# Order of the first loads, the norm's column load, the squares and the warming products at the start of a hybrid decoder block

## The chip, the core and the metric

The kernel runs on one core of a Trainium2 chip. The metric is the device time of one execution in microseconds (us); lower is better. The engines are named as in the profile: PE (TensorE) does the matrix products and PEld its weight loads, DVE (VectorE) and ACT (ScalarE) the elementwise work, POOL (GpSimd) some copies and fills, and SP (SyncE) issues the DMA transfers.

## The reference, cut to what matters

One decoder block over 512 tokens of width 1024, all in float32. Only its beginning is touched by the change:

```
h = rms_norm(x, attn_norm_g)         # x * rsqrt(mean(x*x) + eps) * g
u = h @ w_in
u_sb, u_rw, u_gate = split(u)
q, k, v = heads of u_sb              # 8 heads of 64
o_sb = stick_breaking_attention(q, k, v)
o_rw = rwkv7_time_mix(u_rw, ...)
x = x + (sigmoid gates of u_gate, o_sb @ w_up_sb, o_rw @ w_up_rw) @ w_out
x = x + square(relu(rms_norm(x) @ w_ff1)) @ w_ff2
x = x + sigmoid(rms_norm(x) @ w_ple_gate) * (p @ w_ple_proj)
return rms_norm(x, final_norm_g)
```

## The kernel before, in words

**Products.** Activations lie with the features on the partitions: x is eight tiles of 128 features by 512 tokens, `x_in`. Every float32 operand is cut into two parts, a rounded one (`w_hi`, `h_hi`) and the rest (`w_lo`, `h_lo`). A product over one tile of 128 features is three matmuls, hi by hi (L191), lo by hi (L192) and hi by lo (L193), each 128x128 by 512 columns; `mm3` records them. A unit is 128 output features, so eight tiles and 24 matmuls. ACT makes the hi part of a weight unit (L175, or L221 in `split`), DVE the lo part (L176, or L222).

**The norm.** x is not normalized before the products. `h` is x times the norm's gain (`attn_g`, one of the columns in the small table `cols`), made by ACT (`h_hi`, L348) and DVE (`h_lo`, L349). The factor `rs`, one over the root of the mean square per token, is applied behind the products. For it ACT squares the eight x tiles (L227, L230), DVE adds them up into `ssum` (L232, L234), PE sums over the partitions (L258), ACT does Ln, Exp and Square (L248 to L250), and DVE two more steps (L251, L252). Every `projected` unit (L389, L401, L409) multiplies by `rs`.

**The start.** Warming products on a zeroed tile (L331) keep PE occupied while the first data come. `first_weights(i, part)` loads half a unit of weights and splits it; `first_x(k)` loads one x tile and makes h of it. The first two units, q and k of the first pair of heads, advance together, tile by tile, into two PSUM tiles of the pool `ps_m`. Unit three, v of the first pair, goes into `ps_z`. Units four to six are q, k and v of the second pair. `fetch_to` loads and splits the units that follow; two raw buffers (`w_raw`) and three split ones are in turn, so a load waits until DVE has made the lo part of the unit two before it. Then the transposes of v (L416), the scores (L453 to L455), and for each block of scores the softplus on ACT and DVE: Abs (L458), Exp (L459), Ln (L460), a DVE step (L461), and the split into `sph` and `spl` (L221, L222). Sums over these (L500, L504), an exponential (L505) and the product with v (L492) follow. Projections of later heads are laid between these steps.

**What sets the order.** The program is written in one order, but a scheduler decides the order in which each engine's queue gets its instructions, by their priority and by when its own model has them ready; each engine then works through its queue in that order. `tc.issue_after(x)` puts what its block records behind x on x's engine. All transfers were issued by SP. Eight semaphores are in turn for them, so the ninth waits until the first has landed.

Of the kernel before, what the change touches and what calls it, by code (L numbers as in the profile page):

```python
# [18 lines left out]
P = 128  # L19
T = 512  # L20
D = 1024
KT = D // P
# [63 lines left out]
def tile_block(ctx: ExitStack, tc: tile.TileContext, xT, xt, pT, wts, lora, cols_d, gfin_d, consts_d, out, dbg=None):  # L86
    nc = tc.nc
    act, dve, pool, pe, sync = nc.scalar, nc.vector, nc.gpsimd, nc.tensor, nc.sync
# [3 lines left out]
    def r32(ap):  # L92
        return ap.bitcast(F32)
# [12 lines left out]
    cols = const.tile([P, NCOLS], F32, name="cols")  # L106
# [12 lines left out]
    def col(name, i):  # L119
        return cols[:, COLS[name] + i:COLS[name] + i + 1]  # L120
# [43 lines left out]
    def fetch_to(n, ahead=0):  # L164
        while state["i"] < min(n, len(seq)):
            i = state["i"]
            state["i"] += 1
            load_to(i + 1 + ahead)
            raw = loaded[i] if seq[i][0] != U_FF2 else sources[seq[i]]()
            if seq[i] in homes:  # L170
                hi, lo = homes[seq[i]]()
            else:
                hi = wpool.tile([P, 1024], F32R, name="w_hi")
                lo = wpool.tile([P, 1024], F32R, name="w_lo")
            act.copy(out=hi, in_=raw)  # L175
            dve.tensor_tensor(out=lo, in0=raw, in1=r32(hi), op=ALU.subtract)  # L176
            ready.setdefault(seq[i], []).append((hi, lo))
# [46 lines left out]
    def sum_squares(pool_, src, k, ssum):  # L224

        if k == 0:
            act.activation(out=ssum, in_=src, func=AF.Square)  # L227
            return
        sq = pool_.tile([P, T], F32, name="sq", bufs=2)[:, 0:src.shape[-1]]
        act.activation(out=sq, in_=src, func=AF.Square)  # L230
        if k == 1:
            dve.scalar_tensor_tensor(out=ssum, in0=sq, scalar=NORM_EPS * D / P, in1=ssum, op0=ALU.add, op1=ALU.add)  # L232
        else:
            dve.tensor_tensor(out=ssum, in0=ssum, in1=sq, op=ALU.add)  # L234
# [36 lines left out]
    psm = ctx.enter_context(tc.tile_pool(name="psm", bufs=2, space=PSUM))  # L271
    with ExitStack() as sA:
        h_hi = pa.tile([P, KT, T], F32R, name="h_hi")
        h_lo = pa.tile([P, KT, T], F32R, name="h_lo")
# [41 lines left out]
        with ExitStack() as s1:  # L316
            p1 = s1.enter_context(tc.tile_pool(name="p1", bufs=2))
            ps1 = s1.enter_context(tc.tile_pool(name="ps1", bufs=2, space=PSUM))

            def ps_z():  # L320
                return ps1.tile([P, T], F32, name="ps_z", bufs=5)
# [5 lines left out]
            warm = p1.tile([P, T], BF16, name="warm", tag="sp")  # L327
            pool.memset(warm, 0.0)
            ps = ps_z()
            for _ in range(12):  # L330
                pe.matmul(ps, warm[:, 0:P], warm, start=True, stop=True)  # L331
            sync.dma_start(out=cols, in_=cols_d)
            ssum = p1.tile([P, T], F32, name="ssum", tag="wl")

            raws = [wpool.tile([P, 1024], F32, name="w_raw", bufs=2) for _ in range(2)]
            first_w = [[wpool.tile([P, 1024], F32R, name=n) for n in ("w_hi", "w_lo")] for _ in range(2)]
            xs_in = {}

            def first_weights(i, part):
                cs = slice(part * 512, part * 512 + 512)  # L340
                sync.dma_start(out=raws[i][:, cs], in_=unit(i)[:, cs])
                split(first_w[i][0][:, cs], first_w[i][1][:, cs], raws[i][:, cs])

            def first_x(k):
                x_in = p1.tile([P, 2, T], F32, name="x_in", tag=("sp", "sph", "spl", "wh")[k // 2]) if k % 2 == 0 else xs_in[k - 1][0]
                sync.dma_start(out=x_in[:, k % 2, :], in_=xT[:, k, :])
                xs_in[k] = x_in, x_in[:, k % 2, :]
                act.activation(out=h_hi[:, k, :], in_=xs_in[k][1], func=AF.Copy, scale=col("attn_g", k))  # L348
                dve.scalar_tensor_tensor(out=h_lo[:, k, :], in0=xs_in[k][1], scalar=col("attn_g", k), in1=r32(h_hi[:, k, :]),  # L349
                                         op0=ALU.mult, op1=ALU.subtract)  # L350


            first_weights(0, 0)
            first_x(0)
            first_weights(1, 0)
            for k in range(1, 4):
                first_x(k)
            first_weights(0, 1)
            first_weights(1, 1)
            for k in range(4, KT):  # L360
                first_x(k)
            loaded.extend(raws)
            state["i"] = 2
            for i in range(2):
                ready[seq[i]] = [tuple(first_w[i])]
            fetch_to(3)

            for k in range(KT):
                sum_squares(p1, xs_in[k][1], k, ssum)
            sync.dma_start(out=cst, in_=consts_d[:, 0:NCONST])  # L370
            first = p1.tile([P, 4 * P], F32, name="first", tag="sums", bufs=1)
            sync.dma_start(out=first, in_=consts_d[:, NCONST:NCONST + 4 * P])
# [154 lines left out]
            for _ in islice(v, 1):  # L527
# [6 lines left out]
                              op0=ALU.mult, op1=ALU.add)  # L534
# [24 lines left out]
            parts = {g: {} for g in heads_}  # L559
# [12 lines left out]
        with ExitStack() as s2:  # L572
# [421 lines left out]
            for st in range(HP + 1):  # L994
                parts = [(len(FILL[st]) * KT, filling(FILL[st]))]
# [370 lines left out]
```

## Time and profile before

| | |
|---|---|
| median of 3 runs | 873.17 us (872.13, 873.17, 873.87) |
| the profiled execution's own time | 874.59 us |
| its span, first to last instruction | 872.8 us |
| mean granted TensorE clock | 0.995 of full speed |
| bytes moved by DMA | 95.32 MB, 109 GB/s on average |

The profile is of one execution; its times are microseconds from the first instruction. Its page cuts the span into 40 slices of 21.8 us and gives the busy tenths of each engine in each:

```profile
PE   9999999999999999998999999999999999999995
DVE  7899987896979888666834789858985987697666
ACT  7888887735345253524524465344434533453743
```

The first slices are the part that the change touches: there DVE and ACT are the busiest in the program but for a few slices, while PE is full in nearly all. In a row of the timeline stand the start, the time taken (from the first to the end of the last, where equal rows are merged), engine, line, operation, tiles with the written one first, and in brackets the idle time ahead of it on its engine and what ended it. Matmuls overlap: one of 512 columns shows some 0.39 us but the next starts 0.23 us behind it. In the table by stretches come the stretch, its length, busy time and number of instructions of PE, PEld, DVE, ACT and POOL, the granted clock, the DMA share and GB/s.

### The profile page before, as it was taken

The page shows a single profiled execution, that of the slowest core. Times are in us where ns is not written, and L with a number is a line of the kernel's source. Part 1 is how long each engine was busy: PE and PEld are TensorE (multiplying, and loading weights), DVE is VectorE, ACT ScalarE, POOL GpSimd, SP SyncE. Part 2 cuts the span into 40 slices and gives each one's busy share as a digit, 9 for nine tenths or more (in the row PEclk, how much of TensorE's full clock was granted, in tenths as well). Part 3 has the DMA queues.
Part 4 walks back from the last instruction along what each step waited for, and adds up shares of the span by engine and source line. Part 5 has one row for each costly group of instructions (what it writes and reads, how often), then busy time and mean ns, then how long its engine had stood idle before and what let it go on. Part 6 is the DMA issues. An engine that isn't in the chain of part 4 may idle for free.

```text
span 872.8 us, 13418 instructions
## 1 busy us (share of the span) xinstructions
PE 853.0 (98%) x5182; PEld 687.9 (79%) x5182; DVE 676.7 (78%) x1230; ACT 449.3 (51%) x706; POOL 78.7 (9%) x136
## 2 busy tenths in 40 slices
PE   9999999999999999998999999999999999999995
PEld 6778787877777777776888888888888888888885
DVE  7899987896979888666834789858985987697666
ACT  7888887735345253524524465344434533453743
POOL 1432421003202021010000000000000000000000
PEclk9999999999999999999999999999999999999998
DMA  7212113131221225357735621531252044200422
GB/s 269 97 62 72 62 61 103 54 101 47 73 74 61 86 75 176 102 174 266 272 97 170 240 73 34 186 119 49 87 178 97 25 141 149 97 1 0 171 71 97
DMA packets 32272, 95.32 MB, mean 109 GB/s; under 512 B 3664, under 2 KB 3664, under 8 KB 32208
## 3 DMA queue, kind: packets, MB, share of 16 engines
q1 hardware_dynamic: 32208, 94.46, 32.4%
q8 instruction: 41, 0.67, 0.3%
q14 instruction: 23, 0.19, 0.1%
HBM read 83.96 MB, written 10.49 MB: 108 GB/s over the span
## 4 chain that ended last, share of the span: by engine, by line
PE 74%; DVE 13%; ACT 7%; DMA 3%; issue 2%; SPq 0%; ACTq 0%; DVEq 0%
PE ps_m L191 13%; PE ps_m L193 13%; PE ps_m L192 13%; PE ps_m L208 7%; PE ps_m L206 7%; PE ps_m L207 7%; DVE w_lo L176 2%; DMA w_raw<-in_wts_dram 1%; ACT hx L1039 1%; PE ps_o L492 1%; PE ps_g L898 1%; DVE LX L836 1%; PE ps_z L500 1%; PE ps_s L936 1%; PE ps_c L927 1%
## 5 line engine op out<-in xcount | busy, mean ns | idle before, releaser
L175 ACT CAST w_hi<-w_raw 128x1024 fp32r<-128x1024 f32 x94 | 99.0, 1053 | 175.6 <-PE ps_m L192 114.8
L176 DVE TENSOR_TENSOR w_lo<-w_raw,w_hi 128x1024 fp32r<-128x1024 f32 x94 | 115.2, 1225 | 38.2 <-ACT w_hi L175 37.7
L191 PE MATMUL ps_m<-h_hi,w_hi 128*128 128x512 f32 x320 | 130.7, 410 | 0.0
L192 PE MATMUL ps_m<-h_lo,w_hi 128*128 128x512 f32 x320 | 128.9, 403 | 0.0
L193 PE MATMUL ps_m<-h_hi,w_lo 128*128 128x512 f32 x320 | 127.6, 399 | 0.0
L191 PE MATMUL ps_m<-hx,w_hi 128*128 128x512 f32 x256 | 99.7, 390 | 0.4 <-ACT hx L1039 0.4
L192 PE MATMUL ps_m<-hx,w_hi 128*128 128x512 f32 x256 | 99.6, 390 | 0.0
L193 PE MATMUL ps_m<-hx,w_lo 128*128 128x512 f32 x256 | 99.5, 389 | 0.0
L193 PEld LDWEIGHTS ps_m<-h_hi,w_lo 128*128 128x128 f32 x320 | 60.3, 188 | 11.7
L192 PEld LDWEIGHTS ps_m<-h_lo,w_hi 128*128 128x128 f32 x320 | 60.5, 189 | 11.3 <-DVE h_lo L349 1.1
L191 PEld LDWEIGHTS ps_m<-h_hi,w_hi 128*128 128x128 f32 x320 | 60.7, 190 | 10.5 <-ACT h_hi L348 0.4
L191 PEld LDWEIGHTS ps_m<-hx,w_hi 128*128 128x128 f32 x256 | 48.0, 188 | 10.4 <-ACT hx L1039 0.6
L192 PEld LDWEIGHTS ps_m<-hx,w_hi 128*128 128x128 f32 x256 | 48.1, 188 | 10.2 <-DVE hx L1040 0.2
L193 PEld LDWEIGHTS ps_m<-hx,w_lo 128*128 128x128 f32 x256 | 48.1, 188 | 9.9
L206 PE MATMUL ps_m<-w_hi,fS 128*128 128x512 f32 x128 | 49.8, 389 | 0.0
L207 PE MATMUL ps_m<-w_lo,fS 128*128 128x512 f32 x128 | 49.8, 389 | 0.0
L208 PE MATMUL ps_m<-w_hi,fS 128*128 128x512 f32 x128 | 49.8, 389 | 0.0
L208 PE MATMUL ps_m<-w_hi,fA 128*128 128x512 f32 x96 | 37.3, 389 | 0.0
L206 PE MATMUL ps_m<-w_hi,fA 128*128 128x512 f32 x96 | 37.3, 389 | 0.0
L207 PE MATMUL ps_m<-w_lo,fA 128*128 128x512 f32 x96 | 37.3, 389 | 0.0
L221 ACT CAST fS<-sums 128x256 fp32r<-128x256 f32 (+1 forms) x32 | 19.9, 620 | 33.3 <-DVE sums L1131 33.3
L1204 DVE TENSOR_TENSOR xs<-ps_m,xs 128x512 f32<-128x512 f32 x56 | 35.8, 681 | 0.0
(378 smaller groups left out, 1876.0 us busy)
## 6 DMA issues: line engine op xcount, KB each, us to landing
w_raw<-in_wts_dram SPq DMA_DIRECT2D x98, 512.0 KB, 3.4
gates<-gg SPq DMA_DIRECT2D x16, 256.0 KB, 2.0
x_in<-in_xT_dram SPq DMA_DIRECT2D x8, 256.0 KB, 5.1
tmp<-gates SPq DMA_DIRECT2D x8, 256.0 KB, 4.2
upsb<-tmp SPq DMA_DIRECT2D x8, 256.0 KB, 2.8
ga<-upsb SPq DMA_DIRECT2D x8, 256.0 KB, 6.3
gb<-gates SPq DMA_DIRECT2D x8, 256.0 KB, 5.8
xs<-in_xt_dram SPq DMA_DIRECT2D x4, 512.0 KB, 7.8
```

Source lines behind the costliest of these rows:

```text
L175: act.copy(out=hi, in_=raw)
L176: dve.tensor_tensor(out=lo, in0=raw, in1=r32(hi), op=ALU.subtract)
L191: pe.matmul(ps, wh, xh[:, k, t], start=first, stop=False)
L192: pe.matmul(ps, wh, xl[:, k, t], start=False, stop=False)
L193: pe.matmul(ps, wl, xh[:, k, t], start=False, stop=last)
L206: pe.matmul(ps, xh[:, k + j], wh, start=first and j == 0, stop=False, skip_group_check=True)
L207: pe.matmul(ps, xh[:, k + j], wl, start=False, stop=False, skip_group_check=True)
L208: pe.matmul(ps, xl[:, k + j], wh, start=False, stop=last and j == 1, skip_group_check=True)
L221: act.copy(out=hi, in_=src)
L492: pe.matmul(ps_o[:, j * P:T], vv[:, j, hh, :, :].rearrange("p a d -> p (a d)"), part[:, ZB[j]:ZB[j] + ZN[j]], start=j == 2 and part is wh, ...
L500: pe.matmul(zt[b][:, :n], tri, part[:, s:s + n], start=False, stop=False, skip_group_check=True)
L1204: dve.tensor_tensor(out=xb, in0=pss[t2], in1=xb, op=ALU.add)
```

## The change

Six edits, all in the stage that starts the program:

- eight warming products instead of twelve;
- the table of columns is issued by ACT's queue instead of SP's;
- x tile 0 is asked for ahead of the weights; the first two units of weights come as pieces of 2, 2 and 4 tiles (128, 128 and 256 KB) instead of two halves of 256 KB; x tiles 4 and 5, and 6 and 7, come as one transfer each;
- the third unit's load and split (`fetch_to(3)`) is put behind the last h;
- the squares of tiles 0 to 3 are put behind h of tile 5, those of tiles 4 to 7 behind h of tile 7;
- k of the second pair of heads goes into a `ps_z` tile instead of a `ps_m` one.

```
             ps = ps_z()
-            for _ in range(12):
+            for _ in range(8):
                 pe.matmul(ps, warm[:, 0:P], warm, start=True, stop=True)
-            sync.dma_start(out=cols, in_=cols_d)
+            act.dma_start(out=cols, in_=cols_d)
...
-            def first_weights(i, part):
-                cs = slice(part * 512, part * 512 + 512)
+            def first_weights(i, lo, n):
+                cs = slice(lo * P, (lo + n) * P)
...
-            def first_x(k):
+            def first_x(k, n=1):
...
-                sync.dma_start(out=x_in[:, k % 2, :], in_=xT[:, k, :])
...
+                sync.dma_start(out=x_in[:, k % 2:k % 2 + n, :], in_=xT[:, k:k + n, :])
+                for j in range(k, k + n):
+                    xs_in[j] = x_in, x_in[:, j % 2, :]
+                    parts = (act.activation(out=h_hi[:, j, :], ...),
+                             dve.scalar_tensor_tensor(out=h_lo[:, j, :], ...))
+                return parts
...
-            first_weights(0, 0)
             first_x(0)
-            first_weights(1, 0)
-            for k in range(1, 4):
-                first_x(k)
-            first_weights(0, 1)
-            first_weights(1, 1)
-            for k in range(4, KT):
-                first_x(k)
+            for i in range(2):
+                first_weights(i, 0, 2)
+            first_x(1)
+            first_x(2)
+            for i in range(2):
+                first_weights(i, 2, 2)
+            first_x(3)
+            for i in range(2):
+                first_weights(i, 4, 4)
+            h_some = first_x(4, 2)
+            h_last = first_x(6, 2)
...
-            fetch_to(3)
-
+            with tc.issue_after(h_last[0].ins), tc.issue_after(h_last[1].ins):
+                fetch_to(3)
             for k in range(KT):
-                sum_squares(p1, xs_in[k][1], k, ssum)
+                after = h_some if k < 4 else h_last
+                with tc.issue_after(after[0].ins), tc.issue_after(after[1].ins):
+                    sum_squares(p1, xs_in[k][1], k, ssum)
...
-                    ps = psm.tile([P, T], F32, name="ps_m") if (hp, i) > (1, 0) else ps_z()
+                    ps = psm.tile([P, T], F32, name="ps_m") if (hp, i) > (1, 1) else ps_z()
```

From line 378 on, the changed program's lines are 8 higher than those before (L395 becomes L403, L458 L466, L504 L512).

The scheduler's order at three places. First SP's queue at the program's start, where `w_raw` is a raw weight unit, `x_in` an x tile and `cols` the table of columns; before:

```order
L332 DMA cols<-in_cols_dram 128x74
L341 DMA w_raw<-in_wts_dram 128x512
L346 DMA x_in<-in_xT_dram 128x512
L341 DMA w_raw<-in_wts_dram 128x512
L346 DMA x_in<-in_xT_dram 128x512 x3
L341 DMA w_raw<-in_wts_dram 128x512 x2
L346 DMA x_in<-in_xT_dram 128x512 x4
```

and now:

```order
L341 DMA w_raw<-in_wts_dram 128x256
L346 DMA x_in<-in_xT_dram 128x512
L341 DMA w_raw<-in_wts_dram 128x256
L346 DMA x_in<-in_xT_dram 128x512 x2
L341 DMA w_raw<-in_wts_dram 128x256 x2
L346 DMA x_in<-in_xT_dram 128x512
L341 DMA w_raw<-in_wts_dram 128x512 x2
L346 DMA x_in<-in_xT_dram 128x1024 x2
```

The columns have left SP; a piece of weights, half as large, still stands ahead of x tile 0.

Second, ACT around the norm: squares (`sq`), casts of the units that follow (`w_hi`), and the factor `rs`. Before, from the cast of unit three on:

```order
L175 CAST w_hi<-w_raw 128x1024
L230 ACTIVATE sq<-x_in 128x512 x2
L175 CAST w_hi<-w_raw 128x1024
L248 ACTIVATE rs<-ps_z 128x512
L249 ACTIVATE rs<-rs 128x512
L175 CAST w_hi<-w_raw 128x1024
L250 ACTIVATE nt<-rs 128x512
L175 CAST w_hi<-w_raw 128x1024
```

and now, from the cast of unit four on:

```order
L175 CAST w_hi<-w_raw 128x1024
L230 ACTIVATE sq<-x_in 128x512 x2
L175 CAST w_hi<-w_raw 128x1024
L230 ACTIVATE sq<-x_in 128x512
L175 CAST w_hi<-w_raw 128x1024
L248 ACTIVATE rs<-ps_z 128x512
L249 ACTIVATE rs<-rs 128x512
L250 ACTIVATE nt<-rs 128x512
```

The casts of units five and six now stand ahead of the first step of `rs`; one of them stood between its steps and one behind them. On DVE all seven additions into `ssum` stand behind the last `h_lo`, with the lo parts of units three, four and five among them; three of them stood among the `h_lo` before. On PE, L258 stood behind the seventh product of unit three and stands behind all 24 of it now.

Third, ACT at the first head's scores, in three blocks of 256, 512 and 512 columns (`sp` holds them, `sph` is the hi part). Before:

```order
L458 ACTIVATE sp<-ps_z 128x256
L459 ACTIVATE sp<-sp 128x256
L458 ACTIVATE sp<-ps_z 128x512
L460 ACTIVATE sp<-sp 128x256
L459 ACTIVATE sp<-sp 128x512
L395 CAST qq_407<-qT 64x512
L460 ACTIVATE sp<-sp 128x512
L221 CAST sph<-sp 128x256
L395 CAST qq_408<-qT 64x512
L458 ACTIVATE sp<-ps_z 128x512
L221 CAST sph<-sp 128x512
L221 CAST sums_hi<-sums 128x128
```

and now, behind the three steps of the block of 256 columns:

```order
L466 ACTIVATE sp<-ps_z 128x512
L403 CAST qq_407<-qT 64x512
L221 CAST sph<-sp 128x256
L467 ACTIVATE sp<-sp 128x512
L403 CAST qq_408<-qT 64x512
L468 ACTIVATE sp<-sp 128x512
L466 ACTIVATE sp<-ps_z 128x512
L467 ACTIVATE sp<-sp 128x512
L468 ACTIVATE sp<-sp 128x512
L221 CAST sph<-sp 128x512
L221 CAST sums_hi<-sums 128x128
```

The last block's Exp and Ln now stand ahead of the cast of `sph` of the block before it. On PE, two products of unit six now stand between the transposes of v and the scores, and unit five's 24 products, all but one of which stood behind the scores before, now all stand there.

More of the change, by code (lines that the diff above doesn't have):

```diff
@@ L337, in tile_block @@
             xs_in = {}
-            def first_weights(i, part):
-                cs = slice(part * 512, part * 512 + 512)
+            def first_weights(i, lo, n):
+                cs = slice(lo * P, (lo + n) * P)
                 sync.dma_start(out=raws[i][:, cs], in_=unit(i)[:, cs])
                 split(first_w[i][0][:, cs], first_w[i][1][:, cs], raws[i][:, cs])
-            def first_x(k):
+            def first_x(k, n=1):
                 x_in = p1.tile([P, 2, T], F32, name="x_in", tag=("sp", "sph", "spl", "wh")[k // 2]) if k % 2 == 0 else xs_in[k - 1][0]
[L346 to L350, printed above, removed]
-            first_weights(0, 0)
-            first_x(0)
-            first_weights(1, 0)
-            for k in range(1, 4):
-                first_x(k)
-            first_weights(0, 1)
-            first_weights(1, 1)
-            for k in range(4, KT):
-                first_x(k)
+                sync.dma_start(out=x_in[:, k % 2:k % 2 + n, :], in_=xT[:, k:k + n, :])
+                for j in range(k, k + n):
+                    xs_in[j] = x_in, x_in[:, j % 2, :]
+                    parts = (act.activation(out=h_hi[:, j, :], in_=xs_in[j][1], func=AF.Copy, scale=col("attn_g", j)),
+                             dve.scalar_tensor_tensor(out=h_lo[:, j, :], in0=xs_in[j][1], scalar=col("attn_g", j), in1=r32(h_hi[:, j, :]),
+                                                      op0=ALU.mult, op1=ALU.subtract))
+                return parts
+            first_x(0)
+            for i in range(2):
[9 more added lines that the diff above has]
+            h_last = first_x(6, 2)
             loaded.extend(raws)
```

## The prediction

> **What bounds the kernel now.** I read the page first, for the share of each engine, then the table by stretches, then the timeline of the first 40 us, since the edits end there.
>
> ```profile
> span 872.8 us, 13418 instructions
> PE 853.0 (98%) x5182; PEld 687.9 (79%) x5182; DVE 676.7 (78%) x1230; ACT 449.3 (51%) x706; POOL 78.7 (9%) x136
> ...
> PE 74%; DVE 13%; ACT 7%; DMA 3%; issue 2%; SPq 0%; ACTq 0%; DVEq 0%
> ```
>
> PE (TensorE) is the bound: 98% busy, 74% of the chain that ended last. So a time saved at the start counts if PE runs its products earlier and nothing later makes it wait for the difference.
>
> ```profile
> 50.00:60.00 10.00, 10.00 (x57) 8.42 (x55) 8.93 (x19) 7.52 (x15) 1.72 (x4) 1.00 0.14 54
> ```
>
> From 50 us on PE has no idle time (10.00 of 10.00 us), and behind that point the changed program's order on the engines is the old one. The change is therefore worth what PE gains or loses in the first 50 us. This is what they look like:
>
> ```profile
> 0.73 1.28 ACT L124 ACT_TABLE_LOAD   x1 [0.73 <-PEq L1358]
> 1.18 0.42 SPq L341 DMA_DIRECT2D w_raw<-in_wts_dram  x1
> 1.31 5.30 PE L331 MATMUL ps_z<-warm 128*128 128x512 bf16 x12 [1.31 <-POOL warm L328]
> 1.65 0.42 SPq L346 DMA_DIRECT2D x_in<-in_xT_dram  x1
> 2.14 0.15 PEld L331 LDWEIGHTS <-warm 128*128 128x128 bf16 x1 [0.28 <-issue]
> 2.57 0.15 PEld L331 LDWEIGHTS <-warm 128*128 128x128 bf16 x1 [0.28 <-issue]
> 5.14 0.72 ACT L348 ACTIVATE h_hi<-x_in,cols 128x512 fp32r<-128x512 f32 x1
> 6.05 0.99 PE L191 MATMUL ps_m<-h_hi,w_hi 128*128 128x512 f32 x1
> 7.18 0.40 PE L193 MATMUL ps_m<-h_hi,w_lo 128*128 128x512 f32 x1
> 7.41 0.39 PE L191 MATMUL ps_m<-h_hi,w_hi 128*128 128x512 f32 x1
> 12.96 0.19 PEld L192 LDWEIGHTS ps_m<-h_lo,w_hi 128*128 128x128 f32 x1 [0.43 <-DVE h_lo L349]
> 18.12 0.39 PE L191 MATMUL ps_z<-h_hi,w_hi 128*128 128x512 f32 x1
> ```
>
> The warming products are 0.43 us apart (weight loads at 2.14 and 2.57); from 7.2 us on a product takes 0.23 us from start to start (7.18, 7.41). So TensorE runs at half pace until about 7.0 us. The first real product starts at 6.05, once h_hi of tile 0 is made (5.14 + 0.72 = 5.86); the 48 products of the first two units then run with one notable wait (0.43 us for h_lo at 12.96), and unit three starts at 18.12.
>
> **The change, part by part.** *Start.* On SP a piece of weights still goes ahead of x, against what the change says of itself, but the columns are gone, so x tile 0 is issued one slot (0.47 us: 1.18 to 1.65) earlier, and 128 KB less go before it.
>
> ```profile
> 9.00:10.00 1.00, 1.00 (x6) 0.83 (x5) 1.00 (x3) 1.00 (x3) 0.00 (x0) 1.00 1.04 371
> ...
> cols<-in_cols_dram SPq DMA_DIRECT2D x1, 37.0 KB, 1.9
> x_in<-in_xT_dram SPq DMA_DIRECT2D x8, 256.0 KB, 5.1
> ```
>
> At 371 GB/s these 128 KB are 0.35 us. Tile 0 had landed by 5.14 at the latest, so it lands by 5.14 - 0.47 - 0.35 = 4.3; h_hi takes 0.72, and PE followed it by 0.19 (5.86 to 6.05): first product at 5.25 instead of 6.05. The columns now wait on ACT for the table load (to 2.01) and take 1.9 us: 3.95, in time. Bounds: were they issued during the load, 2.6; were they queued behind the SP transfers like an x tile (5.1), 7.2, and the first product 2 us late. I take 3.95, the row of the same transfer. Eight warming products end at 1.31 + 8 x 0.43 = 4.75 and leave PE idle for 0.5 us; twelve would have held it until 6.4. With the clock released at 7.0 as before, 4 products run at 0.43 until then, and the other 44 take 44 x 0.227 = 10.0: unit three starts near 17.1, which is **1.05 us early** (the wait at 12.96 goes, since no square stands ahead of the last operands on ACT or DVE). Smaller pieces cost a slot each on SP (two more weight pieces), taken back by two x pairs; casts of the same bytes add about 0.1 us each, hidden because PE is behind the operands from tile 1 on. Bounds of this term: 0 (columns or transfers late) to 1.4.
>
> *Norm.* Seven additions into ssum, three of which stood among the operands, now all stand behind the last h_lo on DVE.
>
> ```profile
> 15.41 0.68 DVE L234 TENSOR_TENSOR ssum<-ssum,sq 128x512 f32<-128x512 f32 x1
> 16.02 0.22 DVE L532 CAST ident_b<-cst 128x128 bf16<-128x128 f32 x1
> 16.15 1.21 DVE L176 TENSOR_TENSOR w_lo<-w_raw,w_hi 128x1024 fp32r<-128x1024 f32 x1
> 17.29 0.68 DVE L234 TENSOR_TENSOR ssum<-ssum,sq 128x512 f32<-128x512 f32 x1
> 18.87 0.69 DVE L234 TENSOR_TENSOR ssum<-ssum,sq 128x512 f32<-128x512 f32 x1
> 19.71 1.03 PE L258 MATMUL ps_z<-ssum,cst 128*128 128x512 f32 x2
> 20.78 0.60 ACT L248 ACTIVATE rs<-ps_z 128x512 f32<-128x512 f32 x1 [1.15 <-PE ps_z L258]
> 24.87 0.69 DVE L252 SCALAR_TENSOR_TENSOR rs<-nt,rs 128x512 f32<-128x512 f32 x1
> 25.05 1.05 ACT L175 CAST w_hi<-w_raw 128x1024 fp32r<-128x1024 f32 x1 [1.55 <-DMA w_raw<-in_wts_dram]
> 27.28 0.68 DVE L389 SCALAR_TENSOR_TENSOR qT<-ps_m,rs 128x512 f32<-128x512 f32 x1
> 29.22 0.66 PE L416 MATMUL ps_m<-cst,vT 128*128 128x128 f32 x4 [0.29 <-DVE vT L409]
> ```
>
> An addition advances DVE by 0.61 (15.41 to 16.02), a w_lo by 1.14 (16.15 to 17.29), a small cast by 0.13. h_lo of tile 7 should end at 14.3 (it ended at 15.49). Seven additions, three w_lo and five small casts stand from there to the last addition: 4.3 + 3.4 + 0.7 = 8.4, so ssum is done at 22.8 instead of 19.56. PE gets to L258, now behind all 24 products of unit three, at 17.1 + 24 x 0.227 = 22.5, and starts it at 23.0: a **wait of 0.5 us**, with unit four queued behind it. Then ACT: the cast that waited for its DMA at 25.05 used to stand behind L248 and now stands ahead of it.
>
> ```profile
> 20.99 3.99 DMA w_raw<-in_wts_dram
> ...
> w_raw<-in_wts_dram SPq DMA_DIRECT2D x98, 512.0 KB, 3.4
> ```
>
> Its buffer comes free with the second full w_lo at 19.8 (its DMA was issued at 20.99 before); 3.4 us of transfer and 1.03 of cast bring L248 to 24.2, just behind L258's end at 24.0. From L248's start to rs it was 4.8 us with a cast between; without it, 5 instructions of 0.6 to 0.7 make 3.4: rs at 27.6, 2 us late. But qT had waited until 27.28 behind a w_lo, which now comes earlier: it starts at 27.6 and the transposes of v at 29.7, where PE, with all of unit four done by 29.2, waits 0.5. The same wait is in the row at 29.22 (0.29, counted from the end of the product before; about 0.45 by the pace). This term is **0** (bounds 0 and 1.0, the latter by 3.99 instead of 3.4 and an equal slip of the scores). The third pair's partial sums in ps_z instead of ps_m give PE two products ahead of the scores.
>
> *Scores.* The first head's softplus now runs in another order on ACT.
>
> ```profile
> 31.44 0.36 PE L453 MATMUL ps_z<-qq,kk 128*128 128x256 f32 x1 [0.17 <-DVE kk L405]
> 33.66 0.62 ACT L459 ACTIVATE sp<-sp 128x512 f32<-128x512 f32 x1
> 34.69 0.63 ACT L460 ACTIVATE sp<-sp 128x512 f32<-128x512 f32 x1
> 36.91 0.62 ACT L221 CAST sph<-sp 128x512 fp32r<-128x512 f32 x1
> 37.01 0.47 PE L191 MATMUL ps_m<-h_hi,w_hi 128*128 128x512 f32 x1
> 37.58 0.33 PE L504 MATMUL ps_z<-sph,neg 128*128 128x128 f32 x1
> ```
>
> From the first score to the cast of block 1 it was 5.5 us (31.44 to 36.91). Now Exp and Ln of the last block (0.62 and 0.63, dependent) stand ahead of this cast: some 6.8 us, so 31.7 + 6.8 + 0.6 = 39.1. Ahead of PE's row at L504 (L512 now) stand 20 products and some 4,200 columns of scores and sums, 1.9 us at 0.227 per 512: 31.7 + 4.5 + 1.9 = 38.1. It waits about 1.0 where it waited 0.34 (37.01 to 37.58 for one product); the later blocks slip with it, some 0.3 more. **Loss 1.0** (0.3 to 1.3).
>
> Sum: -1.05 + 0.5 + 0 + 1.0 = +0.45 us. The profiled execution took 874.59 (span 872.8 and 1.8 around it): 875.0. The median of the runs, 873.17, lies 1.4 below this execution, so the same sum gives 873.6.
>
> [...] The rows show half pace until 7.0 us, 5.7 us after the first warming product, and a later return to it:
>
> ```profile
> 403.00:406.40 3.40, 1.31 (x7) 0.88 (x7) 3.16 (x10) 0.64 (x1) 0.00 (x0) 1.00 0.59 217
> 406.40:409.80 3.40, 3.40 (x9) 2.64 (x8) 2.26 (x4) 0.75 (x2) 0.00 (x0) 0.50 0.74 233
> ```
>
> After a stretch with PE busy 1.31 of 3.40 us the granted clock was 0.50 for 3.4 us, then full again. [...]
>
> **Rivals.** (1) *The clock stays at half pace for another 3.4 us*, because the stretch from 3.6 to 7.0 us now has 0.5 us of idle PE in it. Against it: 85% busy; for it: from 0.2 to 3.6 us PE was busy for 67% and the pace stayed low. Eight products instead of 15 run in it, 7 x 0.227 = 1.6 us lost, of which the 0.5 us wait at L258 takes in part: +1.1, 874.7. (2) *Slower: the norm hangs on the weight DMA.* Every us by which the transfer ahead of L248 takes over 3.4 moves rs, qT and the scores, with PE stopped at the transposes. It decides the sign from 4.7 us (0.45 + 1.3 = 1.75); 3.99 was seen, and 6.7 for a transfer of that size queued behind others, but this one is alone in its queue. At 5 us: 875.2. (3) *PE has cover after all*: the scores' new order costs nothing, since more products of units four to six lie between: -1.05 + 0.5 - 0.4 = -0.95, 872.2. (4) *The start isn't gained*: columns or transfers as late as before, PE at unit three at 18.1; L258's wait goes with it: +0.5 on the forecast, 874.1.
>
> **How the numbers follow.** Forecast 873.6 with 0.55 (its own terms give 872.8 to 874.5), rival 1 with 0.12, rival 2 with 0.08, rival 3 with 0.15, rival 4 with 0.10. The three runs before spread over 1.74 us, 0.2%, about what a measurement of this kernel can tell from no change: the bounds are 871.4 and 874.9. Faster: a third of rival 3 and the forecast's edge, 0.07. Slower: rival 2 and a part of 1, 0.13. Same: 0.80. The range, from rival 3 to rival 2, is 872.0 to 875.3.
>
> **What would show it.** In the changed kernel: first L191 at 5.2 (right) or past 6 (rival 4); pace 0.23 from 7.0 or only from 10.4 (rival 1); the first product of unit three at 17.1; a PE wait for DVE ssum at L258 of about 0.5; L248 right behind a cast that waited for its DMA; a PE wait for ACT sph at L512 near 38 to 39. The prediction is wrong if L258 or L512 doesn't wait, or if PE at 50 us stands over 1.5 us away from the old order's place.

## The result, and the profile after

| | before | changed |
|---|---|---|
| median of the runs | 873.28 us | 877.71 us |
| lowest and highest | 872.13, 874.53 | 874.80, 881.72 |
| runs | 15 | 15 |
| the profiled execution | 874.59 us, clock 0.995 | 874.80 us, clock 0.997 |

The changed kernel takes 1.0053 of the time before, 95% interval 1.0043 to 1.0063: 4.4 us slower, outside the predicted range. Its runs spread over 6.9 us, three times as far as those before, and the execution that was profiled is the fastest of them. So the first thing to see is that this profile, taken alone, hides most of the loss. The page of the changed kernel (span, busy times, the queue of instruction fetches, and the chain that ended last):

```profile
span 872.9 us, 13417 instructions
PE 851.9 (98%) x5178; PEld 687.5 (79%) x5178; DVE 678.5 (78%) x1232; ACT 450.6 (52%) x708; POOL 78.7 (9%) x136
...
q8 instruction: 41, 0.67, 0.3%
...
PE 73%; DVE 13%; ACT 7%; DMA 3%; issue 2%; SPq 0%; POOL 0%; ACTq 0%; DVEq 0%
```

Its busy times differ from those before by 0.3% at most. In the stretch from 50 to 60 us PE is busy for 9.56 of 10.00 us, where it was busy all the time before: it waits 0.41 us at 51.35. The stretch, and the timeline of the start, the norm, the first scores and the place near 300 us, with the rows that answer to those in the prediction:

```profile
50.00:60.00 10.00, 9.56 (x49) 7.39 (x50) 9.40 (x18) 7.32 (x14) 3.15 (x5) 1.00 0.17 54
```

```profile
0.73 1.28 ACT L124 ACT_TABLE_LOAD   x1 [0.73 <-PEq L1366]
0.76 0.40 ACTq L332 DMA_DIRECT2D cols<-in_cols_dram  x1
4.25 0.72 ACT L349 ACTIVATE h_hi<-x_in,cols 128x512 fp32r<-128x512 f32 x1 [0.73 <-DMA x_in<-in_xT_dram]
5.02 1.22 PE L191 MATMUL ps_m<-h_hi,w_hi 128*128 128x512 f32 x2
17.67 0.39 PE L191 MATMUL ps_z<-h_hi,w_hi 128*128 128x512 f32 x1
23.59 1.13 PE L258 MATMUL ps_z<-ssum,cst 128*128 128x512 f32 x2 [0.32 <-DVE ssum L234]
23.88 1.05 ACT L175 CAST w_hi<-w_raw 128x1024 fp32r<-128x1024 f32 x1 [2.01 <-DMA w_raw<-in_wts_dram]
24.83 0.59 ACT L248 ACTIVATE rs<-ps_z 128x512 f32<-128x512 f32 x1
39.23 0.60 ACT L221 CAST sph<-sp 128x512 fp32r<-128x512 f32 x1
39.88 0.33 PE L512 MATMUL ps_z<-sph,neg 128*128 128x128 f32 x1 [0.32 <-ACT sph L221]
51.35 0.33 PE L512 MATMUL ps_z<-spl,neg 128*128 128x128 f32 x1 [0.41 <-DVE spl L222]
57.91 0.60 PE L424 MATMUL ps_m<-cst,vT 128*128 128x128 f32 x4
297.34 0.75 PE L820 MATMUL ps_g<-LX,own 32*32 32x32 f32 x64
299.10 0.85 PE L820 MATMUL ps_g<-LX,LB 32*32 32x64 f32 x42
301.56 0.53 PE L820 MATMUL ps_g<-LX,LB 32*32 32x64 f32 x22 [1.60 <-issue]
```

The same late instructions before:

```profile
56.60 0.60 PE L416 MATMUL ps_m<-cst,vT 128*128 128x128 f32 x4
295.97 0.75 PE L812 MATMUL ps_g<-LX,own 32*32 32x32 f32 x64
297.74 1.10 PE L812 MATMUL ps_g<-LX,LB 32*32 32x64 f32 x64
405.09 0.63 PE L979 MATMUL ps_c<-cst,y 128*128 128x128 f32 x4 [2.87 <-DVE y L974]
```

How to read the two together: the lines from 378 on are 8 higher in the changed kernel, so L416 and L424, L812 and L820, L979 and L987 are the same instructions. PE reaches the transposes of the second pair's v at 57.91 instead of 56.60, 1.31 us late, and 64 small products (L820) at 299.10 instead of 297.74, 1.36 us late: nothing is lost or won for 240 us between. They belong to a burst of small products that begins at 297.34, with `own`. Then, inside the group of 64 identical products, PE stands still for 1.60 us, waiting for no other engine ("issue"). Before, the same 64 products ran without a gap. The table of PE's waits in the changed kernel has this stop first:

```profile
PE ps_g L820 <- issue: 1.8, 2, 1.6
...
PE ps_c L987 <- DVE y L982: 1.5, 1, 1.5
...
PE ps_z L512 <- DVE spl L222: 0.4, 1, 0.4
...
PE ps_z L258 <- DVE ssum L234: 0.3, 1, 0.3
PE ps_z L512 <- ACT sph L221: 0.3, 1, 0.3
```

And the second row takes time back: PE waits 1.5 us for y at L987 where it waited 2.87, so that much of its lateness is hidden there.

What stands near 299 us besides is a fetch on the queue `q8 instruction`. The DMA view of the changed kernel for the stretches 293 to 297 and 297 to 301 us (queue, packets, MB, share of 16 engines) has only data in the first and one fetch of 16,384 bytes in the second:

```profile
q1 hardware_dynamic: 250, 0.63, 40.2%
...
q1 hardware_dynamic: 144, 0.52, 41.8%
q8 instruction: 1, 0.02, 1.4%
```

Before, one such fetch stands in the first stretch, at 293.22 us in the trace:

```profile
q1 hardware_dynamic: 188, 0.44, 36.3%
q8 instruction: 1, 0.02, 1.8%
```

Another stands in the second, at 299.00. Over the whole trace of the changed kernel the queue has 41 such fetches (0.67 MB), on average 254 PE instructions apart, with gaps from 117 to 451. That they bring PE's code is inferred from how PE goes on behind them (below). The sixteenth, at 293.22 before, comes at 299.24 in the changed kernel, where PE is 1.36 us late.

### The profile page after: what moved, and what is told of

It is laid out like the page before. It is cut to its first block, busy times and chain, and to the rows that moved or that the text cites. A ratio compares the mean times of both kernels' runs of the same rounds, so it can differ in the third digit from the quotient of the medians.

```text
span 872.9 us, 13417 instructions
## 1 busy us (share of the span) xinstructions
PE 851.9 (98%) x5178; PEld 687.5 (79%) x5178; DVE 678.5 (78%) x1232; ACT 450.6 (52%) x708; POOL 78.7 (9%) x136
## 4 chain that ended last, share of the span: by engine, by line
PE 73%; DVE 13%; ACT 7%; DMA 3%; issue 2%; SPq 0%; POOL 0%; ACTq 0%; DVEq 0%
PE ps_m L191 13%; PE ps_m L193 13%; PE ps_m L192 13%; PE ps_m L208 7%; PE ps_m L206 7%; PE ps_m L207 7%; DVE w_lo L176 2%; DMA w_raw<-in_wts_dram 1%; ACT hx L1047 1%; ACT w_hi L175 1%; PE ps_o L500 1%; PE ps_g L820 1%; PE ps_z L508 1%; PE ps_g L906 1%; DVE LX L844 1%
## 5 line engine op out<-in xcount | busy, mean ns | idle before, releaser
L191 PE MATMUL ps_m<-h_hi,w_hi 128*128 128x512 f32 x312 | 127.7, 411 | 0.3 <-ACT h_hi L349 0.2
L192 PE MATMUL ps_m<-h_lo,w_hi 128*128 128x512 f32 x312 | 125.8, 403 | 0.1
L193 PE MATMUL ps_m<-h_hi,w_lo 128*128 128x512 f32 x312 | 124.7, 400 | 0.0
L192 PEld LDWEIGHTS ps_m<-hx,w_hi 128*128 128x128 f32 x256 | 48.1, 188 | 10.2 <-DVE hx L1048 0.2
```

The costliest lines, as they stand in the source:

```text
L191: pe.matmul(ps, wh, xh[:, k, t], start=first, stop=False)
L192: pe.matmul(ps, wh, xl[:, k, t], start=False, stop=False)
L193: pe.matmul(ps, wl, xh[:, k, t], start=False, stop=last)
```

## The experiments

Three theories stood at the start. **F**: four warming products fewer are eight PE instructions fewer (a weight load and a product each), which shifts where PE's code is fetched against the bursts of small products. **C**: the shorter warming lets the clock be released later or fall back. **S**: the new order around norm and scores costs all of it.

**Warming and number of instructions, crossed.** `a12` is the changed kernel with twelve products:

```
-            for _ in range(8):
+            for _ in range(12):
```

> The changed kernel with twelve warming products instead of eight; nothing else moves on any engine. Measured so far: 877.7 median for the changed kernel, 873.3 for the one before; by their two profiles PE is 1.3 us late from 51 to 298 us, then a further 1.6 us in a burst of small products (L820) where PE waited for nothing but its own instructions. Theory F (instruction fetch: eight PE instructions fewer shift the borders at which PE's code comes in into bursts of small products): the late fetch goes, median 875 +- 0.7. Theory C (clock: with eight products the clock is released a window later in many executions, or half-pace windows come back): that goes, 875 +- 0.7 too, the profile's release near 7.0, and the granted clock of all timed runs 0.995 or more. Theory S (the new order around norm and scores costs it all): 877.5 +- 0.7.

`a8t4` keeps eight and adds four small ones, so that the number of instructions is that of twelve; `b8` and `b8t4` do to the kernel before what the change did to it, without and with the four small ones:

```
             for _ in range(8):
                 pe.matmul(ps, warm[:, 0:P], warm, start=True, stop=True)
+            for _ in range(4):
+                pe.matmul(ps[:, 0:16], warm[:, 0:P], warm[:, 0:16], start=True, stop=True)
```

> The changed kernel with its eight warming products and four more of 16 columns behind them: as many PE instructions as with twelve, but 0.3 us or less of PE's time. Theory F: as with twelve, 875 +- 0.7, and no stop of PE in the burst at L822. Theory C: the clock is as with eight, 877.5 +- 0.7, clocks of the timed runs down to 0.992. Theory S: 877.5 +- 0.7.

> The kernel before with eight warming products instead of twelve; nothing else moves. Theory F: the borders of PE's code shift as in the changed kernel, 1.5 to 3 us more: 875 to 876.3, with a stop of PE inside a burst of small products. Theory C: PE idles from 4.7 to 6.0 us, the clock is released later: 875 to 877, clocks of the timed runs below 0.995 in some. Theory S: 873.3 +- 0.5.

> The kernel before with eight warming products and four of 16 columns behind them: PE's instructions as many as before, the warming as short as in the changed kernel. Theory F: 873.3 +- 0.5. Theory C: 875 to 877, as with eight alone. Theory S: 873.3 +- 0.5.

`a8long` is the cell that was missing: a warming as long as twelve products in as few instructions as eight. A float32 product of 512 columns shows as two records that start 0.44 us apart (L258 before, at 19.71 and 20.15), where the products around it are 0.23 us apart.

```
-            for _ in range(8):
+            warm32 = p1.tile([P, T], F32, name="warm32", tag="sph")
+            pool.memset(warm32, 0.0)
+            for _ in range(4):
                 pe.matmul(ps, warm[:, 0:P], warm, start=True, stop=True)
+            for _ in range(2):
+                pe.matmul(ps, warm32[:, 0:P], warm32, start=True, stop=True)
```

> The changed kernel with a warming as long as twelve products made of fewer instructions: four bf16 products and two f32 ones of 512 columns (which take two passes of twice the length), so that PE is busy to about 6.5 us, but as many PE instructions stand ahead of the first real product as with eight. Theory F (only the place of the code borders counts): as the changed kernel, 877 +- 1, with PE's stop of 1.5 to 2.2 us in the burst at L820 near 299 us. Theory C (the short warming and PE's idle time behind it count): as with twelve, 874 +- 0.6, no stop.

Measured (each ratio to the kernel before on the same chip, whose median lay between 872.2 and 874.2 from one such comparison to the next, so kernels of different rows are compared by ratio; stop: the `issue` wait in the burst near 299 us):

| kernel | instructions ahead | warming | median us | ratio, 95% interval | stop |
|---|---|---|---|---|---|
| changed | 8 fewer | short | 877.71 | 1.0053, 1.0043 to 1.0063 | 1.60 |
| a8t4 | as before | short | 874.30 | 1.0012, 1.0002 to 1.0022 | none |
| a12 | as before | long | 873.87 | 1.0005, 0.9997 to 1.0014 | none |
| a8long | 8 fewer | long | 876.39 | 1.0045, 1.0029 to 1.0060 | 2.0 |
| b8 | 8 fewer | short | 876.95 | 1.0046, 1.0027 to 1.0064 | 1.97 |
| b8t4 | as before | short | 874.47 | 1.0014, 1.0004 to 1.0024 | none |

The time goes with the number of instructions, in both programs, and much less with the warming. By the ratios eight fewer cost 0.41% in the changed program, some 3.6 us, and 0.32%, some 2.8 us, in the one before. Four products' worth of warming costs 0.07% in the first, where the intervals overlap, and 0.14% (1.4 us by the medians) in the second. Theory S falls as the cause of the loss: with twelve products the whole new order is within the measurement of no change. Theory C falls as its main cause, since `a8long` loses about as much with the long warming and `a8t4` little with the short one. F's own numbers were met in `a8t4` and `a8long` and missed elsewhere: `a12` came out 0.4 us under the least that F or C gave, `b8` 0.65 over F's most, within C's range, and `b8t4` 0.7 over F's most. So the warming has a part. In the ten traces with twelve products the clock was released (its first record at full speed) between 5.2 and 7.3 us, in `a8long` at 5.8; with eight it was released at 10.2 and 10.3 us in two of seven (`b8t4` and one execution of the changed kernel), and in `b8` it fell back to half from 8.00 to 11.41 us. In `a12` the burst is one group again, and its fetch is in the first stretch, as before. The timeline of PE and the DMA view from 293 to 297 us of `a12`:

```profile
299.57 1.10 PE L820 MATMUL ps_g<-LX,LB 32*32 32x64 f32 x64
```

```profile
q1 hardware_dynamic: 268, 0.72, 45.5%
q8 instruction: 1, 0.02, 2.0%
```

**Why the changed kernel's other runs are slower still.** Two more executions of it, unchanged:

> The changed kernel itself once more, to see where one of its slower executions loses time against the profiled one (874.8). Theory F: the stop near 299 us comes again and others stand at fetches elsewhere, late ones above all. Theory C: the clock is released near 10 us or falls back to half pace for 3.4 us, 1.4 to 1.7 us each; then the granted clock shows where.

> As the look before it, a third execution: 876 to 880. Theory F: same stop near 299 us. Theory C: a half-pace window in the granted clock that the profiled execution did not have.

They took 877.24 and 877.61 us. Both have the stop, of 2.05 and 1.98 us, and both lose more right behind it. The table by stretches of the second (PE's busy time is the second figure; the clock is the third from the end), with the row in the timeline where PE goes on:

```profile
302.73 0.64 PE L820 MATMUL ps_g<-LX,LB 32*32 32x64 f32 x22 [1.98 <-issue]
```

```profile
299.60:303.02 3.42, 1.44 (x76) 1.21 (x73) 0.93 (x2) 1.16 (x2) 0.00 (x0) 1.00 0.12 46
303.02:306.43 3.41, 3.41 (x74) 2.30 (x66) 1.95 (x4) 1.58 (x2) 0.00 (x0) 0.50 0.08 28
```

the first:

```profile
300.43:303.84 3.41, 1.36 (x72) 1.10 (x66) 0.74 (x2) 1.16 (x2) 0.00 (x0) 1.00 0.09 31
303.84:307.25 3.41, 3.41 (x78) 2.38 (x69) 1.95 (x4) 1.57 (x2) 0.00 (x0) 0.50 0.14 50
```

and the profiled execution from the result, whose clock stayed full:

```profile
296.93:300.35 3.42, 3.02 (x141) 2.40 (x140) 1.58 (x5) 1.12 (x2) 0.00 (x0) 1.00 0.51 158
300.35:303.76 3.41, 2.20 (x71) 1.61 (x72) 2.31 (x5) 1.24 (x3) 0.00 (x0) 1.00 0.02 5
```

The stretches are cut at the release of the clock in each execution (6.06, 10.29 and 6.83 us) and multiples of 3.413 us behind it: a half-clock window was that long before (406.39 to 409.80) and here (303.02 to 306.43, 303.84 to 307.25), and these three began 117, 87 and 86 such lengths behind their releases. Where the stop falls into one window, PE is busy in it for 1.36 or 1.44 us and gets the half clock for the next window, which costs about another 1.1 us of PE's time (the lateness against the kernel before grows from 4.40 to 5.50 us). Where the border of two windows cuts the stop, as in the profiled execution, PE is still busy for 2.20 us of 3.41 in the emptier one, and nothing follows. So in these three executions the half clock came behind the stop, and whether it came went with where the windows lay: by that reading it is a part of the spread from 874.8 to 881.7. The 15 runs go the same way: the seven with a mean clock of 0.996 or 0.997 took 874.80 to 877.71, the seven with 0.992 to 0.994 took 877.72 to 881.72.

**How the fetch comes late.** Two conjectures were set against each other: PE's sequencer reads some instructions ahead and stops at the wait ahead of the burst before it has asked for the code, which is all or nothing (R); or every instruction of shift costs a part (G). `a8t2` is `a8t4` with two small products, `b12t4` the kernel before with four behind its twelve, eight instructions more:

> The changed kernel with two products of 16 columns behind its eight: four PE instructions more than the changed kernel, four fewer than with twelve products. In the kernels that ran well the burst near 297 us began 22 to 28 PE instructions behind the one that PE was starting when the code was fetched near 295 us; with eight fewer it would begin 14 to 17 behind. Theory R (PE's sequencer reads ahead by some 17 to 22 instructions, stops at the burst's wait, and the fetch goes out only when that wait ends): here it is 18 to 21, at the limit; either no stop and 874.3 +- 0.7, or the stop and 877 +- 1, with the fetch at 295 or 299 us to match, and nothing between. Rival G (each instruction fewer costs a part, by contention spread over all fetches): halfway, 875.7 +- 0.4.

> The kernel before with four products of 16 columns behind its twelve: eight PE instructions more, the shift to the other side. Theory R: the fetch near 293 us goes out in the stretch of long products as before, 30 to 36 instructions ahead of the burst; 873.3 +- 0.7, no stop near 297 us. Rival G (any shift from the old alignment costs): 875 to 877.

`a8t2` took 877.93 us, 1.0042 (1.0029 to 1.0055), with the whole stop; `b12t4` 872.28 us, 0.9980 (0.9971 to 0.9990), with none. Of `a8t2`:

```profile
302.26 0.54 PE L822 MATMUL ps_g<-LX,LB 32*32 32x64 f32 x24 [1.61 <-issue]
```

Half the shift costs all of it, and a shift to the other side costs nothing, so G falls. Counted in the traces, the fetch goes out when PE starts the instruction 21 or 23 ahead of the burst's first (L820 with `own`, which waits for DVE and PE) in all twelve traces without a stop, those with eight instructions more among them; in the six with a stop it comes 192 to 276 instructions behind the burst's first, and nothing lies between. In the profiled changed kernel the burst starts at 297.34, a weight transfer of 512 KB runs from 297.55 to 299.65, and the fetch is seen at 299.24. So the fetch is seen either 21 or 23 instructions ahead of the burst or 1.73 to 2.36 us behind its first product, with the burst already running, as R has it; where the border of the code lies no trace shows.

Two more things in the six fit that PE stands still for this code: it goes on 2.3 to 2.4 us behind the start of the fetch in each, and 4,245 PE instructions stand ahead of the place where it stopped (4,247 in `b8`), in `a8t2` too, whose burst begins four instructions later. One number of R was missed: it had the fetch of `b12t4` 30 to 36 instructions ahead of the burst, and it came 21 ahead, as without the eight more. So eight instructions more did not move its place against the burst. In the twelve it stands 0.93 to 1.20 us behind PE's small product at L927 (by the lines of the kernel before), which also waits for a semaphore and is 34 instructions ahead of the burst; in the six it stands 1.73 to 2.36 us behind the burst's own first product. That speaks for R's account, in which the end of a wait lets the fetch go, in both cases; the reading ahead itself is not shown. How much of the delay is the transfer's no run tells, since none moved it. The stop of 1.6 to 2.1 us stands beside the 1.10 us that all 64 products take without it.

**What of the order costs, and what hides it.** Two parts of the change undone in `a12`: `a12sq` records the squares as before, `a12ps` has k of the second pair in `ps_m` again.

```
-                after = h_some if k < 4 else h_last
-                with tc.issue_after(after[0].ins), tc.issue_after(after[1].ins):
-                    sum_squares(p1, xs_in[k][1], k, ssum)
+                sum_squares(p1, xs_in[k][1], k, ssum)
```

```
-                    ps = psm.tile([P, T], F32, name="ps_m") if (hp, i) > (1, 1) else ps_z()
+                    ps = psm.tile([P, T], F32, name="ps_m") if (hp, i) > (1, 0) else ps_z()
```

> The changed kernel with twelve warming products and the squares recorded as before (not put behind h): shows in the trace how much of the 1.9 us by which PE is late from 55 us on is theirs. If the squares' place is the cause, PE stands within 0.5 us of the kernel before at 60 us; if it is the two PSUM tiles or the fetch, it stays at 1.5 to 2.

> The changed kernel with twelve warming products and k of the second pair back in a ps_m tile: the other part. If the PSUM tile is the cause, PE is within 0.5 us of the kernel before at 60 us; if the squares' place is, it stays at 1.5 to 2 us.

One execution each took 872.79 and 875.78 us. Their starts differ (unit three at 19.10 and 18.73; the three of the changed kernel differ by 1.3 us there), so PE's way from unit three to the transposes of the second pair's v is compared. Before it is 18.12 to 56.60 (38.48 us), in the changed kernel 17.67 to 57.91 (40.24), in `a12` 18.32 to 58.52 (40.20), in `a12sq` 19.10 to 57.41 (38.31) and in `a12ps` 18.73 to 59.88 (41.15). So the order costs 1.7 to 1.8 us there, and without the squares' place nothing is left of it. Other traces bear that out: the two further programs with the squares as before (`a12sqy`, `a12sqyt`, below) have 38.31 and 38.16, the five others with the order of before 37.87 to 38.82, the other two executions of the changed kernel 40.27 and 40.81. The 0.9 us by which `a12ps` is longer don't show that the PSUM tile helps: `a8long`, which has the tile, took 41.49, and 1.4 us of `a12ps` are a wait for `ssum` at L258.

These 1.8 us do not reach the end in `a12` (1.0005). The wait for y at L979 was meant to show why: ACT's copies of y stand there behind sigmoids that wait for their DMAs (in the kernel before ACT is idle for 4.32 us ahead of L662 at 388.38). `by` (from the kernel before) and `a12y` (from `a12`) put the copies ahead:

```
-                    act.copy(out=y[HALVES[odd]], in_=psy[odd]...)
+                    copy = act.copy(out=y[HALVES[odd]], in_=psy[odd]...)
+                if hp == HP - 1:
+                    state["norm"] = copy
```

> The kernel before, with ACT's copies of the last y (L958) put ahead of the two sigmoids of tmp (L662) and the one of gb (L1075), which wait there for their DMAs; PE's order is untouched. In the kernel before, PE stands still for 2.9 us at L979 for y. Theory H (what is lost before 400 us is hidden by this wait, since y hangs on these DMAs and not on PE): the copy goes early, the wait shrinks by 2 us or more, 870.5 to 871.8 against 873.2. Rival N (y hangs on PE's own chain, the wait stays): 873.2 +- 0.5.

> The changed kernel with twelve warming products and the same move of y's copies. With twelve products PE was 1.9 us late from 55 to 298 us and yet the time came out 0.8 above the kernel before or less. Theory H: with the wait for y gone the 1.9 us count: 1.5 to 2.2 us above the kernel before with the same move. Rival N: as far apart as without the move, 0.4 to 0.8.

`by` took 872.68 us, 0.9991 (0.9981 to 1.0001), `a12y` 874.12 us, 1.0006 (0.9994 to 1.0017). In `by` the wait has shrunk by 2.5 us, as H said:

```profile
404.41 0.63 PE L981 MATMUL ps_c<-cst,y 128*128 128x128 f32 x4 [0.38 <-DVE y L976]
```

0.38 us of it are left. The gain of 0.7 us is half of the least that H forecast, and its interval reaches no change; the two kernels now stand 1.4 us apart where `a12` and the kernel before stood 0.8: in the direction of H, below its 1.5, and within the intervals of either. That the wait hides lateness is shown by the traces alone (2.87 us before, 1.46 in the changed kernel, 0.73 in `a12`); that it hides all of the 1.8 us is not settled.

**A version that beats both.** `a12sqy` joins `a12sq` and the moved copies. `byt` and `a12sqyt` are `by` and `a12sqy` with four small products more.

> A version meant to beat both: the changed kernel with twelve products, the squares as before, and the last y's copies put ahead of the sigmoids on ACT. The look at the kernel with the squares alone gave 872.8, with PE 0.8 us late at 55 us after a late start. Without a stop and with the wait for y shortened: 872.0 to 872.8, 0.7 to 1.3 under the kernel before. If the wait for y only moves on, 872.8 to 873.3.

> The kernel before with both moves that helped it: four products of 16 columns behind the twelve (0.998 of the kernel before by itself) and the last y's copies ahead of the sigmoids (0.999). If the two add up: 0.9965 to 0.9975. If one covers the other (with the code fetch on time PE is back at the wait for y): 0.998.

> The best version so far (the changed kernel with twelve products, the squares as before, the last y's copies moved: 0.9979 of the kernel before) with the same four small products behind the twelve. If the shift helps here as it did the kernel before: 0.9965 to 0.9975. If its gain there was the wait for y, which is gone here already: 0.998.

`a12sqy` took 872.34 us, 0.9979 (0.9969 to 0.9988), `byt` 872.14 us, 0.9987 (0.9975 to 0.9999), `a12sqyt` 871.39 us, 0.9978 (0.9968 to 0.9988). The gains don't add up: what `b12t4` won alone (0.9980) is not won again on top of the moved copies, and neither `byt` nor `a12sqyt` came to the 0.9965 to 0.9975 that a sum would have given. The best are 0.2% under the kernel before: the changed kernel with its first loads and PSUM tile, but twelve warming products, the squares where they were, and y's copies moved.

## Why the prediction was wrong

Forecast 873.6, range 872.0 to 875.3; measured 877.71.

- **The step that failed**: "behind that point the changed program's order on the engines is the old one. The change is therefore worth what PE gains or loses in the first 50 us." The order is the old one, but not the place of the program in PE's stream of code: with eight instructions fewer in the first microseconds a fetch 300 us later stood in a burst (299.24) and no longer in a stretch of 0.23 us products (293.22 before). The prediction counted four warming products as 1.7 us of PE's time and never as instructions. It failed a second way too, with the other sign: at L987 the wait for y hides lateness of the first 400 us (1.46 us are left of 2.87), so a term of the first 50 us is not worth its size at the end.
- **Start, -1.05**: -0.45 in the profiled execution (17.67 against 18.12), +0.88 and -0.21 in the other two. The first product came at 5.02, even before the forecast 5.2, but 0.3 us of the lead was lost among the first products, which ran at half pace (0.43 us from 6.04 to 6.47, 0.23 from 7.11 on), one of them after a wait of 0.2 us for `h_lo`, and more at the x pairs near 12 us. The columns didn't wait for ACT's table load (0.73 to 2.01): ACT's queue issued them at 0.76, as the bound that was put aside had it. They took 2.5 us, not 1.9, and landed at about 3.3, with no effect, since x tile 0 landed last (`h_hi` waited for it until 4.25). Two casts of 256 columns took 0.80 us on ACT (0.41 and 0.39) where one of 512 took 0.62.
- **Clock** (rival 1, 0.12): released at 6.83 in the profiled execution, but at 10.29 in one of the other two, with unit three 1.3 us later. There the idle time was longer than the 0.5 us that the prediction had: PE was busy for 2.47 of 3.42 us in the window that ended 3.41 us ahead of the release. That idle time in such a window holds the clock back was the author's conjecture; no run shows it alone. The late release itself came in a part of the executions and has a part in the spread; what the medians showed of the warming is 0.4 us in this program (`a12` against `a8t4`), within the noise.
- **Norm, 0.5**: the wait at L258 is 0.32 and L248 stands right behind the cast that waited for its DMA, at 24.83 (forecast 24.2). Right in the profiled execution; in the other two the wait was 0.4 and 0.9. The 14.3 us at which the last `h_lo` should end was given without its working; it ended at 14.92.
- **Scores, +1.0**: `sph` of the second block ended the wait at 39.88, but for 0.32 us. PE's ten products more ahead of it (2.27 us at 0.227) account for nearly all of 39.88 against 37.58. The longest wait came one block later, at 51.35 for `spl` (0.41), where the prediction had 0.3 for all later blocks. Idle time of PE between unit three and the transposes at 57.91 grew only by 0.53 us (1.36 for 0.83); the rest of the 1.76 is products that start further apart, whose cause was not followed. So the size came out, the place and the mechanism only in part.
- **Sum at 50 us, +0.45**: +1.31 at 57.91, below the 1.5 that was named as the point of failure; the other two executions stand at +2.7 and +2.1, above it. 0.60 of the difference is the start (-0.45 for -1.05), the rest the norm and the scores (1.76 for 1.5).
- **From there to 877.7**: the execution of 877.61 was 2.2 us late ahead of the burst; the stop added 2.2 and the half clock 1.1 (5.5 us in all); the shorter wait for y, 1.69 instead of 2.87, took back 1.2. That leaves 4.3 us at L987, near the 4.4 between the medians. Behind it the profiled execution before loses another 1.6 us in a half-clock window at 406 us (in the prediction's rows), which the changed kernel's three traces don't have. That the median run before is without this window is likely, as it is 1.3 us faster than the profiled one, but no trace shows it.
- **The chances**: "slower by over 0.2%" had 0.13, by a mechanism (the weight DMA) that did not occur: the transfer ahead of L248 took 3.37 us (forecast 3.4).

## What to carry to other kernels

Here four or eight instructions fewer on the engine that is full, in the first microseconds, went with a code fetch near 299 us that came inside a burst, and cost 0.3 to 0.4%. Where a program has bursts of small instructions, look at the waits on "issue" and the fetch queue in that stretch, and judge such an edit only beside a version with the same number of instructions (four tiny products served here). A loss at the start is to be followed to the next place where the full engine waits for another, which can hide it; and a stop of 2 us was followed here by 1.1 us more at the half clock. One profile of a kernel whose runs spread over 0.8% shows one of its cases, here the mildest.

## What the runs showed of the hardware

- A code fetch that came 4.4 to 5.3 us later than elsewhere, counted against the burst, went with a stop of TensorE of 1.6 to 2.1 us within a group of 64 identical products, in all six traces with four or eight instructions fewer ahead, and in none of the other twelve.
- Cut on the grid of each execution's own release, a window with 1.31 us of busy PE (before, in the prediction's rows), with 1.36 and with 1.44 was followed by a half clock for 3.41 us. A window with 1.51 in `a8t2` and one with 1.69 in `b8` were not. But in `b8` a window with 1.68, the first behind the release, was, so in these traces busy time alone doesn't draw the line. The two of `b8` that differ, each with the window behind it:

```profile
4.58:8.00 3.42, 1.68 (x5) 0.70 (x5) 1.68 (x3) 2.69 (x5) 0.00 (x0) 1.00 0.89 303
8.00:11.41 3.41, 3.41 (x9) 2.41 (x9) 3.35 (x6) 3.41 (x7) 0.00 (x0) 0.50 1.04 391
...
298.10:301.50 3.40, 1.69 (x75) 1.46 (x71) 1.43 (x3) 1.16 (x2) 0.00 (x0) 1.00 0.30 116
301.50:304.90 3.40, 3.14 (x93) 2.35 (x93) 2.49 (x6) 1.66 (x2) 0.00 (x0) 1.00 0.02 5
```

- The first release came behind a window with 3.27 us of busy PE or more in all 18 traces, and not behind one with 2.75 (`b8t4`) or 2.47 (the changed kernel's execution with the release at 10.29).
- ACT issued a DMA at 0.76 us, 0.03 us behind the start of its table load (0.73) and ahead of its end (2.01).
- Why the kernel before runs 0.2% faster with eight instructions more (`b12t4`, whose wait for y was 1.09 us) stays open. A part may be the clock: none of its 11 runs had a mean clock under 0.996, and 9 of the 23 runs of the kernel before beside it had 0.994 or 0.995.
